# A gated DeltaNet block on one Trainium2 core: half-block norms, query norms and substitution rows issued at other places

## The chip, the core and the metric

The kernel runs on one core of one Trainium2 chip. The engines are TensorE (PE in the profile; its weight loads are PEld), VectorE (DVE), ScalarE (ACT), GpSimd (POOL) and SyncE (SP, which here issues most transfers). The metric is the device time of one execution in microseconds.

## The reference

One decoder layer over 2048 tokens of width 1024: RMS norm, a gated DeltaNet mixer of 8 heads of width 128, then a squared-ReLU MLP of width 4096, and a final norm. All in float32. The mixer, cut to what matters:

```python
proj = h @ w_in
qkv = silu(causal_depthwise_conv(proj[..., :3 * W], conv_w))       # 4 taps
q, k = l2_normalize(q), l2_normalize(k)                            # per head
beta = sigmoid(b);  g = -exp(a_log) * softplus(a + dt_bias)
# per head, chunks of 64 tokens, gc = cumsum(g) in the chunk
lower = strict_lower(einsum(k*beta, k) * decay)
u, w  = triangular_solve(lower + I, [v*beta, k*beta*exp(gc)])
attn  = causal(einsum(q, k) * decay)
for each chunk:                                                    # state S of 128 x 128
    v_new = u - w @ S
    o     = (q*exp(gc)) @ S + attn @ v_new
    S     = S * exp(g_last) + (k*exp(g_last - gc)).T @ v_new
o = rms(o) * norm_w * silu(z);  out = o @ w_out
```

## The kernel before

The tokens are worked in two blocks (`blk`) of 1024, each as two half blocks (`s`) of 512. A half block does the mixer for the 8 heads in four pairs (`h` = 0, 2, 4, 6); after both half blocks follow the out projection and the MLP of the block, which the change does not touch. So there are 16 pairs in all.

Float32 products run as three matmuls on high and low parts (L117 to L119), so a projection (`conv_part`) is 24 matmuls of 128x512. Weights are split on GpSimd (L90, L91) in block 0. A pair runs six projections (k, q, v for two heads, counted by `n`), each followed by its causal convolution on VectorE (L307, L311) with copies on ScalarE (L303, L304, L310). Between the projections stand steps of two pairs at once:

- For the pair itself: after n = 3 and 4 the key products (`key_matrices`, L429 to L439, tiles mt), then `invert_diagonal`: ScalarE copies four pieces of the triangular matrices into xc (L322), VectorE transposes them into pr (L325) and then substitutes row by row, 31 rows, each a multiply (L333, tmp) and a reduction (L335, tt). These rows are taken from a generator, `rows_of`, a few at a time.
- For the pair before (`prev`): `prepare2`, a generator of stages taken one by one through `next(stages)`. It inverts the triangular matrices from the 32-wide diagonal blocks up (`invert`: tr L345 is VectorE's transpose of the finished rows, tcm L347, then L365 to L394 on TensorE), then makes k and v per token (kt, vt: transposes L469 into po, ScalarE L472) and the attention matrix (L478, L480).

After the six projections `wind_up` does the rest of the pair before: two gate projections (z), the query norms (`query_norms`: squares sq on ScalarE L450, sums on TensorE L452, an addition n on VectorE L454), and `chain`, four steps of the state for two heads: k·S (L496), y (VectorE, L498), q·S (L502, into po), y times the inverse (L505), vr (ScalarE, L507), the state's update (L511, S L512), L515. Calls of `fill` in it take rows of `rows_of`, to fill VectorE's time.

During the first half block of a block, each pair also loads and norms one 128-row tile of the next half block's input (`norm_transpose`): the load xt, its squares on ScalarE, the reciprocal root on VectorE (`rstd_of`), the scaling xn (L181), then eight transposes on TensorE (L186, po) with high and low parts hh and hl.

The code states an order, but a scheduler then orders the instructions of each engine, and an engine takes its own strictly in that order. The three PSUM tags matter: kq and pj with three buffers, po with two. Four buffers (tag "xt") serve xt, xn, xc, pr and a gate's z2.

Of the kernel before, what the change touches and what calls it, by code (L numbers as in the profile page):

```python
# [16 lines left out]
P = 128  # L17
# [16 lines left out]
def tile_kernel(ctx: ExitStack, tc: tile.TileContext, x, w_in, w_out, w_up, w_down, n_mlp, n_fin, consts, out):  # L34
# [106 lines left out]
    def rstd_of(ssq, use_pool=False):  # L141

        n = ssq.shape[-1]
        m = sm.tile([P, n], F32, name="rm", tag=f"rm{n}")
        dve.tensor_scalar(m, ssq, 1.0 / D, EPS, op0=MULT, op1=ADD)  # L145
        r = sm.tile([P, n], F32, name="rst", tag=f"rst{n}", bufs=3)
        if use_pool:
            pool.tensor_tensor(r, m, mhalf, op=ALU.pow)
        else:
            rsqrt(r, m)  # L150
        return r
# [22 lines left out]
            dve.scalar_tensor_tensor(hl[:, k, :], ps, nmix[:, k:k + 1], hh[:, k, :].bitcast(F32),  # L174
                                     op0=MULT, op1=SUB)

    def norm_transpose(i, src, xn, wcol, hh, hl, tag):

        ssq = sm.tile([P, 1], F32, name="ssq", tag="ssq", bufs=3)
        act.activation(xn, src, AF.Square, accum_out=ssq)  # L180
        dve.tensor_scalar_mul(xn, src, rstd_of(ssq))  # L181
        ti = slice(i * P, (i + 1) * P)
        for k4 in range(0, KS, 4):
            ps = big(tag)
            for k in range(4):
                pe.transpose(ps[:, k * P:(k + 1) * P], xn[:, (k4 + k) * P:(k4 + k + 1) * P], ident)  # L186
# [259 lines left out]
    def query_norms(ap, u, q2, j):  # L446

        ps = big("kq")
        sq = ap.tile([P, HB], F32, name="sq", tag="scr", bufs=1)
        act.activation(sq, q2[:, j * HB:(j + 1) * HB], AF.Square)  # L450
        for t in range(HT):
            pe.matmul(ps[:, t:t + 1], sq[:, sl(t)], ones[:, 0:1], start=True, stop=True)  # L452
        c = NC + j * HT
        dve.tensor_scalar_add(u["n2"][:, c:c + HT], ps[:, 0:HT], 4.0 * EPS)  # L454

    def prepare2(ap, sb, h, q2, k2, v2, gt, u, ub, t64):

        c0 = h * HT
        dt_, rk = u["dt"], u["rk"]
        yield from invert(ap, u["mt"], u["tt"], ub, t64)  # L460
        yield
        qe = row(ap, eg_d, "qe", sb, c0)
        (dve if c0 == NH * HT - NC and sb % 2 else pool).tensor_tensor(flat(qe), flat(qe), q2, op=MULT)
        kt, vt = head(ap, "kt"), head(ap, "vt")
        for dst, src, sc in ((vt, v2, lambda c: rk[:, c:c + 1]), (kt, k2, lambda c: gt["egl"][:, c0 + c:c0 + c + 1])):
            for hf in range(2):
                ps = big("po")
                for t in range(HT):
                    pe.transpose(ps[:, sl(t)], src[:, sl(hf * HT + t)], ident)  # L469
                for t in range(HT):  # L470
                    c = hf * HT + t
                    act.activation(dst[:, c, :], ps[:, sl(t)], AF.Copy, scale=sc(c))  # L472
        yield
        for hf in range(2):
            ps = big("kq")
            for t in range(HT):
                s = sl(hf * HT + t)
                pe.matmul(ps[:, sl(t)], k2[:, s], q2[:, s], start=True, stop=True)  # L478
            cs = slice(hf * HT, (hf + 1) * HT)
            dve.tensor_tensor(flat(dt_[:, cs, :]), ps, flat(dt_[:, cs, :]), op=MULT)  # L480
        u.update(ub=ub, qe=qe, kt=kt, vt=vt, at=dt_, k2=k2, gt=gt, c0=c0)

    def chain(ap, h0, u, fill):

        def col(name, c):
            return u["gt"][name][:, u["c0"] + c:u["c0"] + c + 1]

        po = [big("po") for _ in range(HP)]
        for t in range(HT):
            ts_ = slice(t * P, (t + 1) * P)  # L490
            cs = [j * HT + t for j in range(HP)]
            st = [S[h0 + j] for j in range(HP)]
            ys, vrs = [], []
            for j, c in enumerate(cs):
                ps = big("kq")
                pe.matmul(ps[:, 0:P], u["k2"][:, c * P:(c + 1) * P], st[j], start=True, stop=True)  # L496
                y = ap.tile([P, P], F32, name="y", tag="y")
                dve.scalar_tensor_tensor(y, ps[:, 0:P], col("neg", c), u["vt"][:, c, :], op0=MULT, op1=ADD)  # L498
                ys.append(y)
            fill(3)  # L500
            for j, c in enumerate(cs):
                pe.matmul(po[j][:, ts_], u["qe"][:, c, :], st[j], start=True, stop=False)  # L502
            for j, c in enumerate(cs):
                ps = big("kq")
                pe.matmul(ps[:, 0:P], u["ub"][:, c, :], ys[j], start=True, stop=True)  # L505
                vr = ap.tile([P, P], F32, name="vr", tag="vr")
                act.activation(vr, ps[:, 0:P], AF.Copy, scale=u["cc"][:, c:c + 1])  # L507
                vrs.append(vr)
            for j, c in enumerate(cs):
                ps = big("kq")  # L510
                pe.matmul(ps[:, 0:P], u["kt"][:, c, :], vrs[j], start=True, stop=True)  # L511
                dve.scalar_tensor_tensor(st[j], st[j], col("egt", c), ps[:, 0:P], op0=MULT, op1=ADD)  # L512
            fill(2)
            for j, c in enumerate(cs):
                pe.matmul(po[j][:, ts_], u["at"][:, c, :], vrs[j], start=False, stop=True)  # L515
        os_ = [ap.tile([P, HT, P], F32, name="o", tag="o") for _ in range(HP)]
        ms = sm.tile([P, NC], F32, name="ms", tag="ms")
        for j in range(HP):
            for t in range(HT):
                c = j * HT + t  # L520
                act.activation(os_[j][:, t, :], po[j][:, t * P:(t + 1) * P], AF.Square, accum_out=ms[:, c:c + 1])
        nq = sm.tile([P, NC], F32, name="nq", tag="nq")
        dve.tensor_scalar_mul(nq, u["n2"][:, NC:2 * NC], EPS * P)
        dve.scalar_tensor_tensor(nq, ms, 1.0 / P, nq, op0=MULT, op1=ADD)
        rq = sm.tile([P, NC], F32, name="rq", tag="rq")
        rsqrt(rq, nq)
        for j in range(HP):
            for t in range(HT):
                c = j * HT + t
                act.activation(os_[j][:, t, :], po[j][:, t * P:(t + 1) * P], AF.Copy, scale=rq[:, c:c + 1])  # L530
        return os_
# [53 lines left out]
    def mixer(blk, hT):  # L585
        with tc.tile_pool(name="ap", bufs=2) as ap:
# [11 lines left out]
            def wind_up(stages, rows_of, sb, h, hT, qkv, gt, u):  # L598

                def fill(n):  # L600
                    for _ in range(n):
                        next(rows_of, None)

                fill(1)
                z = [gate(ap, hT, h, sb)]
                for _ in stages:
                    pass
                z.append(gate(ap, hT, h + 1, sb))
                for j in range(HP):
                    query_norms(ap, u, qkv[0], j)  # L610
                os_ = chain(ap, h, u, fill)
                return [(sb, h + j, os_[j], z[j]) for j in range(HP)]

# [4 lines left out]
            for s in range(2):  # L618
                sb = 2 * blk + s
                for h in range(0, NH, HP):  # L620
                    qkv, n = [], 0
                    stages = stages_of(*prev) if prev is not None else iter(())
                    next(stages, None)
                    if s == 0 and h == 0:
                        hT2 = half_tiles()
                    for part in (1, 0, 2):
                        d = ap.tile([P, HP * HB], F32, name=f"c{part}", tag=f"c{part}")
                        qkv.append(d)
                        for j in range(HP):
                            conv_part(ap, hT, part, h + j, d[:, j * HB:(j + 1) * HB], sb)  # L630
                            n += 1
                            next(stages, None)
                            if s == 0 and h == 0 and n <= 3:
                                if n == 1:
                                    gt = {}
# [12 lines left out]
                            if blk == 0 and s == 1 and n in (2, 5):  # L648
                                split_out(h // HP * 2 + n // 5)
                            if s == 0 and n == 1:  # L650
                                xt = wp.tile([P, D], F32, name="xt", tag="xt", bufs=4)
                                r0 = (sb + 1) * HB + h // HP * P
                                sp.dma_start(xt, x[r0:r0 + P, :])
                            if s == 0 and n == 2:
                                xt_steps = norm_transpose(
                                    h // HP, xt, wp.tile([P, D], F32, name="xn", tag="xt", bufs=4), nmix, *hT2, "po")
                            if s == 0 and n in (2, 4):
                                next(xt_steps)
                            if s == 0 and h == NH - HP and n >= 4:
                                if n == 4:  # L660
# [2 lines left out]
                                next(g_steps, None)  # L663
                    if prev is not None:
                        ready += wind_up(stages, rows_of, *prev)
                    for _ in rows_of:
                        pass
                    prev = sb, h, hT, (qkv[1], qkv[0], qkv[2]), gt, u
                if s == 0:
                    for _ in g_steps:  # L670
# [226 lines left out]
```

## Time and profile before

| | |
|---|---|
| median of 3 runs | 2931.71 us (2922.69 to 2936.09) |
| profiled execution | 2926.04 us, span 2924.3 us |
| mean granted clock of TensorE | 0.978 |
| busy: PE, DVE, ACT, POOL | 95%, 53%, 35%, 25% of the span |
| mixer of block 0 (28 to 655 us) and block 1 (1510 to 2075 us) | PE idle about 78 and 39 us |

Times are microseconds from the span's start. A line of the table of waits reads: engine, tile and line that waited, the engine, tile and line it waited for, then the total, the number of waits and the longest. In a window or timeline row the busy time stands with the number of instructions in brackets; the bracket at the end of a timeline row is the idle time ahead of it and what ended it. `po L186 <- DVE xn L181` is TensorE's transpose of the next half block's tile, which waits for VectorE's scaling.

### The profile page before, as it was taken

What the parts mean: (1) busy time and instruction counts of PE and PEld (TensorE: products, weight loads), DVE (VectorE), ACT (ScalarE), POOL (GpSimd) and SP (SyncE); (2) the same over time, 40 slices, a digit from 0 to 9 for tenths busy, and PEclk for the clock granted to TensorE, in tenths of its full rate; (3) what the DMA queues carried; (4) which work ended last, traced back from release to release, by engine and by line L of the source; (5) the groups of instructions that cost most, each with busy time, mean ns of one, the idle gap of its engine ahead of it and who ended that gap; (6) DMA issues with size and microseconds to landing.
All of it is one profiled execution on the core that took longest, in us unless ns stands there. A gap on an engine that the chain in (4) does not pass through costs nothing.

```text
span 2924.3 us, 40261 instructions
## 1 busy us (share of the span) xinstructions
PE 2768.4 (95%) x15352; PEld 2325.2 (80%) x15352; DVE 1548.9 (53%) x3846; ACT 1034.0 (35%) x2338; POOL 731.9 (25%) x646
## 2 busy tenths in 40 slices
PE   7688989999999999999998999999999999999998
PEld 6577777779888888888886778787888888888887
DVE  7777777763433233333487676766544333332335
ACT  3455555554221211211246655555423112112112
POOL 6334232110042332332211111111004323323321
PEclk9889999999999999999999999999999999999999
DMA  6544455456421111111253434434662111111111
GB/s 227 182 159 168 165 177 176 169 202 226 161 72 43 58 50 38 58 51 37 65 194 142 142 122 145 145 137 148 199 230 87 44 44 58 44 44 58 48 40 65
DMA packets 81842, 337.62 MB, mean 115 GB/s; under 512 B 8817, under 2 KB 17265, under 8 KB 60145
## 3 DMA queue, kind: packets, MB, share of 16 engines
q1 hardware_dynamic: 60528, 292.98, 29.9%
q10 hardware_dynamic: 21120, 42.08, 4.2%
q8 instruction: 120, 1.97, 0.3%
q14 instruction: 74, 0.60, 0.1%
HBM read 271.98 MB, written 63.05 MB: 115 GB/s over the span
## 4 chain that ended last, share of the span: by engine, by line
PE 65%; DVE 10%; ACT 7%; issue 2%; DMA 2%; ACTq 0%; POOL 0%; POOLq 0%; DVEq 0%
PE pj L117 11%; PE pj L118 11%; PE pj L119 11%; PE kq L118 8%; PE kq L119 8%; PE kq L117 8%; ACT xc L322 2%; DVE tmp L333 2%; DVE c L307 1%; DVE tt L335 1%; DMA orw<-o_d 1%; PE kq L505 1%; PE kq L511 1%; PE kq L496 1%; PE kq L429 1%
## 5 line engine op out<-in xcount | busy, mean ns | idle before, releaser
L117 PE MATMUL pj<-hh,w 128*128 128x512 f32 x2048 | 820.7, 401 | 0.7 <-ACT c L304 0.7
L118 PE MATMUL pj<-hh,w 128*128 128x512 f32 x2048 | 817.6, 399 | 0.0
L119 PE MATMUL pj<-hl,w 128*128 128x512 f32 x2048 | 812.5, 397 | 0.0
L119 PEld LDWEIGHTS pj<-hl,w 128*128 128x128 f32 x2048 | 389.6, 190 | 79.0 <-issue 0.6
L117 PEld LDWEIGHTS pj<-hh,w 128*128 128x128 f32 x2048 | 390.1, 190 | 78.2 <-ACT c L304 1.1
L118 PEld LDWEIGHTS pj<-hh,w 128*128 128x128 f32 x2048 | 391.5, 191 | 75.8 <-issue 0.4
L742 ACT ACTIVATE r<-pj 128x512 f32<-128x512 f32 x128 | 76.9, 601 | 1059.7 <-PE pj L119 1059.7
L119 PE MATMUL kq<-dl,uh 128*128 128x512 f32 x992 | 386.8, 390 | 0.0
L118 PE MATMUL kq<-dh,ul 128*128 128x512 f32 x992 | 386.7, 390 | 0.0
L117 PE MATMUL kq<-dh,uh 128*128 128x512 f32 x992 | 386.6, 390 | 0.0
L745 DVE TENSOR_TENSOR ul<-r,uh 128x512 fp32r<-128x512 f32 x128 | 128.7, 1006 | 480.4 <-ACT uh L744 480.4
L785 DVE TENSOR_TENSOR x<-kq,x 128x512 f32<-128x512 f32 x256 | 176.8, 691 | 225.8 <-PE kq L119 223.1
L307 DVE SCALAR_TENSOR_TENSOR c<-raw,cst,c 128x512 f32<-128x512 f32 x288 | 239.9, 836 | 76.9 <-ACT c L304 73.9
L90 POOL TENSOR_SCALAR w<-wr 128x1024 fp32r<-128x1024 f32 x106 | 114.9, 1084 | 602.8 <-PE pj L119 380.5
L91 POOL TENSOR_TENSOR w<-wr,w 128x1024 fp32r<-128x1024 f32 x106 | 263.8, 2489 | 7.1
L785 DVE TENSOR_TENSOR x1h<-kq,x1h 128x512 f32<-128x512 f32 x256 | 176.7, 691 | 155.7 <-PE kq L119 155.4
L90 POOL TENSOR_SCALAR dh<-wr 128x1024 fp32r<-128x1024 f32 x62 | 64.5, 1058 | 642.0 <-PE kq L118 614.3
L117 PEld LDWEIGHTS kq<-dh,uh 128*128 128x128 f32 x992 | 186.2, 188 | 40.4 <-DVE rm L145 1.4
L118 PEld LDWEIGHTS kq<-dh,ul 128*128 128x128 f32 x992 | 186.2, 188 | 39.4
L119 PEld LDWEIGHTS kq<-dl,uh 128*128 128x128 f32 x992 | 186.2, 188 | 38.8
L333 DVE TENSOR_TENSOR tmp<-tt,pr 128x2 f32<-128x2 f32 (+30 forms) x496 | 162.1, 327 | 9.9 <-POOL pr L326 0.5
L117 PE MATMUL pj<-w,hh 128*128 128x256 f32 x512 | 147.2, 287 | 8.2 <-DMA w<-wo 5.9
(305 smaller groups left out, 3840.5 us busy)
## 6 DMA issues: line engine op xcount, KB each, us to landing
w<-wi SPq DMA_DIRECT2D x96, 1024.0 KB, 4.9
wi<-w SPq DMA_DIRECT2D x32, 1024.0 KB, 4.8
wr<-in_w_up SPq DMA_DIRECT2D x64, 512.0 KB, 3.6
w<-wo SPq DMA_DIRECT2D x32, 1024.0 KB, 5.7
wr<-in_w_down SPq DMA_DIRECT2D x64, 512.0 KB, 3.6
wr<-in_w_in SPq DMA_DIRECT2D x32, 512.0 KB, 5.8
qe<-eg_d ACTq DMA_DIRECT2D x16, 512.0 KB, 3.8
o_d<-z2s ACTq DMA_DIRECT2D x32, 256.0 KB, 3.3
```

Source lines behind the costliest of these rows:

```text
L90: pool.tensor_scalar(dst_h, src, 1.0, 0.0, op0=MULT, op1=ADD)
L91: pool.tensor_tensor(dst_l, src, dst_h.bitcast(F32), op=SUB)
L117: pe.matmul(ps, ah, bh, start=first and i == 0, stop=False)
L118: pe.matmul(ps, al, bh, start=False, stop=False)
L119: pe.matmul(ps, ah, bl, start=False, stop=last and i == n - 1)
L307: dve.scalar_tensor_tensor(dst, raw[:, k:k + HB], cw[:, 4 * f + k:4 * f + k + 1], dst, op0=MULT, op1=ADD)
L322: act.copy(xc[r], mt[r, :, 32 * b:32 * b + 32].rearrange("p t i -> p i t").unsqueeze(2) .to_broadcast([32, 32, R, NC]))
L333: dve.tensor_tensor(tmp[:, 0:n, 0:i + 1], tt[:, 0:n, 0:i + 1], pr[:, i, 0:i + 1].unsqueeze(1).to_broadcast([P, n, i + 1]), op=MULT)
L335: dve.tensor_reduce(tt[:, 0:n, i], tmp[:, 0:n, 0:i + 1], axis=mybir.AxisListType.X, op=ADD)
L742: act.activation(r, ps, AF.Relu)
L745: dve.tensor_tensor(ul[:, hs], r, uh[:, hs].bitcast(F32), op=SUB)
L785: dve.tensor_tensor(dst, ps, dst, op=ADD)
```

## The change

Four edits. First, in a block's first half the load of the next half block's tile moves ahead of the pair's first projection; the squares, the root and the scaling follow n = 1 (before, n = 2), and the eight transposes follow n = 3 and 4, four at each (before, n = 2 and 4). In block 1 the root is a power on GpSimd in place of eight operations on VectorE. Second, the query norms move from `wind_up` into `prepare2`, between stages of the inversion. The empty stage between inversion and kt/vt goes, and so does the stage that was taken ahead of the first projection. Third, the first pair's rows are no longer used up at the end of that pair: 12 of them come after the second pair's first projection and 24 more calls after its second (its stages start one projection later). Fourth, the second `fill` in a state step takes three rows instead of two.

```diff
-        dve.tensor_scalar_mul(xn, src, rstd_of(ssq))
+        dve.tensor_scalar_mul(xn, src, rstd_of(ssq, use_pool))
+        yield
...
-        yield from invert(ap, u["mt"], u["tt"], ub, t64)
-        yield
+        for i, _ in enumerate(invert(ap, u["mt"], u["tt"], ub, t64)):
+            yield
+            if i in (1, 2):
+                query_norms(ap, u, q2, i - 1)
...
-            fill(2)
+            fill(3)
...
-                for j in range(HP):
-                    query_norms(ap, u, qkv[0], j)
                 os_ = chain(ap, h, u, fill)
...
-                    next(stages, None)
+                    if s == 0:
+                        xt = wp.tile([P, D], F32, name="xt", tag="xt", bufs=4)
+                        r0 = (sb + 1) * HB + h // HP * P
+                        sp.dma_start(xt, x[r0:r0 + P, :])
...
-                            next(stages, None)
+                            if s == 0 and h == HP and n < 3:
+                                for _ in range(12 * n):
+                                    next(rows_of, None)
+                            if not (s == 0 and h == HP and n == 1):
+                                next(stages, None)
...
-                            if s == 0 and n == 2:
                                 xt_steps = norm_transpose(
-                                    h // HP, xt, wp.tile([P, D], F32, name="xn", tag="xt", bufs=4), nmix, *hT2, "po")
-                            if s == 0 and n in (2, 4):
+                                    h // HP, xt, wp.tile([P, D], F32, name="xn", tag="xt", bufs=4), nmix, *hT2, "po",
+                                    blk > 0)
+                            if s == 0 and n in (1, 3, 4):
                                 next(xt_steps)
...
-                    for _ in rows_of:
-                        pass
+                    if prev is not None:
+                        for _ in rows_of:
+                            pass
```

The lines of the changed kernel lie one to three lower: L333 becomes L334, L335 L336, L450 L451, L452 L453, L454 L455, L472 L475, L496 L499, L498 L501, L505 L508.

How the scheduler then orders the engines is seen at three places. On VectorE, around the second pair of block 0: the scaling xn and the substitution rows of the first pair around it, before:

```order
137 L333 TENSOR_TENSOR tmp<-tt,pr 128x4x14
138 L139 SCALAR_TENSOR_TENSOR rst<-rt,rst 128x1
141 L333 TENSOR_TENSOR tmp<-tt,pr 128x4x15
142 L139 SCALAR_TENSOR_TENSOR rst<-rt,rst 128x1
144 L181 TENSOR_SCALAR xn<-xt,rst 128x1024
145 L333 TENSOR_TENSOR tmp<-tt,pr 128x4x16
```

and now:

```order
120 L334 TENSOR_TENSOR tmp<-tt,pr 128x2x6
121 L139 SCALAR_TENSOR_TENSOR rst<-rt,rst 128x1
124 L181 TENSOR_SCALAR xn<-xt,rst 128x1024
126 L334 TENSOR_TENSOR tmp<-tt,pr 128x2x7
128 L334 TENSOR_TENSOR tmp<-tt,pr 128x2x8
```

The last number of tmp grows by one with each row of the substitution, so xn stood ahead of the row with 16 and now stands ahead of the row with 7.

On VectorE again, in the second half of block 0, at the first state step of the pair h = 0, while the next pair's rows run, before:

```order
865 L333 TENSOR_TENSOR tmp<-tt,pr 128x5x18
866 L454 TENSOR_SCALAR n_3427<-kq 128x4
867 L335 TENSOR_REDUCE tt<-tmp 128x5
868 L333 TENSOR_TENSOR tmp<-tt,pr 128x5x19
869 L537 SCALAR_TENSOR_TENSOR z2s<-z2s,pj 128x512
870 L335 TENSOR_REDUCE tt<-tmp 128x5
871 L454 TENSOR_SCALAR n_3427<-kq 128x4
872 L333 TENSOR_TENSOR tmp<-tt,pr 128x5x20
873 L498 SCALAR_TENSOR_TENSOR y<-kq,neg,vt 128x128 x2
```

and now:

```order
870 L334 TENSOR_TENSOR tmp<-tt,pr 128x5x17
871 L336 TENSOR_REDUCE tt<-tmp 128x5
872 L334 TENSOR_TENSOR tmp<-tt,pr 128x5x18
873 L501 SCALAR_TENSOR_TENSOR y<-kq,neg,vt 128x128
874 L540 SCALAR_TENSOR_TENSOR z2s<-z2s,pj 128x512
875 L501 SCALAR_TENSOR_TENSOR y<-kq,neg,vt 128x128
876 L336 TENSOR_REDUCE tt<-tmp 128x5
```

The additions n are gone from this place; y stands two rows of the substitution further ahead than it did, where n stood.

On ScalarE, ahead of the same state step, the copies xc for the next pair and the vt and kt of this one, before:

```order
311 L322 COPY xc<-mt 32x1024
314 L472 ACTIVATE vt<-po,rk 128x128 x8
315 L472 ACTIVATE kt<-po,egl 128x128 x2
317 L472 ACTIVATE kt<-po,egl 128x128 x6
318 L322 COPY xc<-mt 32x1024
321 L322 COPY xc<-mt 32x1024 x2
```

and now:

```order
317 L475 ACTIVATE vt<-po,rk 128x128 x8
319 L475 ACTIVATE kt<-po,egl 128x128 x8
320 L323 COPY xc<-mt 32x1024 x3
323 L323 COPY xc<-mt 32x1024
```

The four copies xc, the first of which stood ahead of vt and kt, now all stand behind them.

More of the change, by code (lines that the diff above doesn't have):

```diff
@@ L175, in enter_first, with norm_transpose @@
                                      op0=MULT, op1=SUB)
-    def norm_transpose(i, src, xn, wcol, hh, hl, tag):
+    def norm_transpose(i, src, xn, wcol, hh, hl, tag, use_pool=False):
         ssq = sm.tile([P, 1], F32, name="ssq", tag="ssq", bufs=3)
         act.activation(xn, src, AF.Square, accum_out=ssq)
-        dve.tensor_scalar_mul(xn, src, rstd_of(ssq))
+        dve.tensor_scalar_mul(xn, src, rstd_of(ssq, use_pool))
+        yield
         ti = slice(i * P, (i + 1) * P)
@@ L650, in mixer @@
                             if s == 0 and n == 1:
-                                xt = wp.tile([P, D], F32, name="xt", tag="xt", bufs=4)
-                                r0 = (sb + 1) * HB + h // HP * P
-                                sp.dma_start(xt, x[r0:r0 + P, :])
-                            if s == 0 and n == 2:
                                 xt_steps = norm_transpose(
-                                    h // HP, xt, wp.tile([P, D], F32, name="xn", tag="xt", bufs=4), nmix, *hT2, "po")
-                            if s == 0 and n in (2, 4):
+                                    h // HP, xt, wp.tile([P, D], F32, name="xn", tag="xt", bufs=4), nmix, *hT2, "po",
+                                    blk > 0)
+                            if s == 0 and n in (1, 3, 4):
                                 next(xt_steps)
```

## The prediction

> **What bounds the kernel.** I read the page's busy times first, then TensorE's waits, then a table of windows by stage, and last the timelines of two places.
>
> ```profile
> span 2924.3 us, 40261 instructions
> PE 2768.4 (95%) x15352; PEld 2325.2 (80%) x15352; DVE 1548.9 (53%) x3846; ACT 1034.0 (35%) x2338; POOL 731.9 (25%) x646
> PE po L186 <- DVE xn L181: 27.2, 2, 16.0
> PE kq L496 <- DVE n L454: 21.6, 8, 5.5
> PE po L469 <- ACT vt L472: 13.3, 10, 5.1
> PE po L186 <- ACT o L530: 11.6, 4, 8.1
> PE kq L452 <- ACT sq L450: 11.6, 4, 3.2
> 28.00:312.00 284.00, 230.92 (x1375) 188.69 (x1373) 217.50 (x582) 140.16 (x305) 124.92 (x115) 0.89 0.50 174
> 312.00:655.00 343.00, 318.31 (x2037) 267.49 (x2038) 247.28 (x746) 180.59 (x431) 68.19 (x91) 0.96 0.53 181
> 1510.00:1750.00 240.00, 215.00 (x1369) 176.92 (x1367) 173.56 (x584) 140.88 (x310) 29.50 (x62) 0.96 0.41 145
> 1750.00:2075.00 325.00, 311.40 (x2046) 262.34 (x2046) 229.01 (x750) 180.25 (x432) 32.74 (x68) 0.98 0.42 146
> ```
>
> TensorE is busy 95% of the span, so the kernel can only gain where TensorE waits, or where its clock is cut. The waits (total, times, longest) that the change touches are the xn scaling, the query norms n with their squares sq, and o and vt, ScalarE's reads of the po buffers. The four windows (length, then busy PE, PEld, DVE, ACT, POOL, then the granted clock) are block 0's first and second half and block 1's; outside them stands the MLP, which is untouched. TensorE idles 284 − 230.92 = 53 us, 25, 25 and 14: about 117 us in the stages that change. There VectorE is busy 70 to 77%, so a wait on it can be a wait for throughput and not for order.
>
> **A settled pair (second half blocks).** The rows of one pair of block 1, between the fourth projection's end and the first state step:
>
> ```profile
> 1951.31 1.14 PE L392 MATMUL kq<-ub,z 64*64 64x64 f32 x16
> 1959.51 2.01 ACT L322 COPY xc<-mt 32x1024 f32<-32x1024 f32 x1 [3.35 <-DVE mt L439]
> 1962.48 2.09 ACT L472 ACTIVATE vt<-po,rk 128x128 f32<-128x128 f32 x8
> 1965.66 1.65 ACT L472 ACTIVATE kt<-po,egl 128x128 f32<-128x128 f32 x6
> 1967.33 1.99 ACT L322 COPY xc<-mt 32x1024 f32<-32x1024 f32 x1
> 1970.67 4.12 ACT L322 COPY xc<-mt 32x1024 f32<-32x1024 f32 x2
> 1974.83 1.25 DVE L325 STREAM_TRANSPOSE pr<-xc 128x1024 f32<-128x1024 f32 x1 [2.07 <-ACT xc L322]
> 1976.62 0.16 DVE L333 TENSOR_TENSOR tmp<-tt,pr 128x2 f32<-128x2 f32 x1
> 1979.83 0.39 PE L117 MATMUL pj<-hh,w 128*128 128x512 f32 x1
> 1980.06 0.39 PE L118 MATMUL pj<-hh,w 128*128 128x512 f32 x1
> 1982.78 0.95 PE L452 MATMUL kq<-ones,sq 128*128 128x1 f32 x8
> 1985.21 0.16 DVE L454 TENSOR_SCALAR n<-kq 128x4 f32<-128x4 f32 x1
> 1985.42 0.49 PE L496 MATMUL kq<-S,c 128*128 128x128 f32 x2 [1.36 <-DVE n L454]
> 1987.24 0.49 PE L505 MATMUL kq<-y,ub 128*128 128x128 f32 x2 [0.87 <-DVE y L498]
> ```
>
> The order of work before shows why n is late: it stands behind 17 rows of the substitution, from 1976.62 to 1985.21, and these behind pr, which ends the chain of four xc copies on ScalarE. The change takes n away, but in the new order the first y stands behind the same 17 to 18 rows (the fence on VectorE above). So the wait moves from n to y.
>
> Its size: without waits TensorE stood at L496 at 1985.42 − 1.36 = 1984.06, or 32.8 us after 1951.31. In the new order six projection matmuls (1980.06 − 1979.83 = 0.23 each, 1.4) and the two groups of norm sums (0.95 each, about 1.7 with their overlap) no longer stand ahead; the k·S and q·S matmuls (about 1.4) now do. It reaches the y product near 31.1 us. On the other side the first xc copy ran in an idle place of ScalarE (3.35 idle before it) and now stands behind vt and kt; the edit takes away the empty stage that let it in. I add 1.8 of its 2.01 to pr, take off the two n (0.3), and with the rows unchanged y is done about 36.0 us after 1951.31. The wait is 36.0 − 31.1 = 4.8 us instead of 1.36 + 0.87 = 2.2.
>
> A longer gap also costs behind its end (columns as in the windows above):
>
> ```profile
> 565.50:572.00 6.50, 5.74 (x22) 4.83 (x23) 4.73 (x20) 0.73 (x2) 0.00 (x0) 0.51 0.79 268
> 1985.20:1992.00 6.80, 5.71 (x40) 4.97 (x40) 6.35 (x26) 1.47 (x4) 0.00 (x0) 1.00 0.01 4
> ```
>
> The first stretch follows a gap of 3.9 us on n in block 0 (row below), the second the gaps of 1.36 and 0.87. Only the longer gap is followed by half clock; half of 5.74 busy us is about 2.8 us lost, and about 2.4 where the stretch is shorter.
>
> In block 0 GpSimd's weight splits hold VectorE up; the waits of the two second halves, block 0's first, stand behind:
>
> ```profile
> 560.00 2.37 POOL L91 TENSOR_TENSOR w<-wr,w 128x1024 fp32r<-128x1024 f32 x1
> 560.21 2.21 DVE L333 TENSOR_TENSOR tmp<-tt,pr 128x33 f32<-128x33 f32 x1
> ...
> PE kq L496 <- DVE n L454: 11.8, 3, 3.9
> PE kq L365 <- ACT z L367: 3.6, 4, 1.4
> ...
> PE kq L452 <- ACT sq L450: 2.7, 1, 2.7
> PE po L469 <- ACT vt L472: 2.3, 4, 0.6
> PE kq L365 <- ACT z L367: 2.3, 4, 0.7
> ```
>
> A row of some 0.2 us becomes 2.21 while the split runs. With one such stall (and 0.8 of smaller ones) between pr and y, y comes at 38.8 and the wait is 7.5, against 11.8/3 = 3.9 on n and, as in block 1, some 0.8 on y and vt. Against this, the norm sums between the inversion's steps fill the wait on z (0.9 a pair in block 0, 0.6 in block 1). Per settled pair, then: block 0, 7.5 − 4.7 − 0.9 = +1.9, at a clock that was cut before too; block 1, 2.6 − 0.6 (z) − 0.6 (vt) = +1.4, and +2.4 for the half clock that a gap of 4.8 brings and one of 1.36 did not, +3.8. Two pairs are settled in each half. The pair that enters the half I count −0.7 and +2.2 (the same y wait, less the 2.6 or so on sq, which goes), the last two together −0.2 and +0.6. Second halves: 3.8 − 0.7 − 0.2 = +2.9 and 7.6 + 2.2 + 0.6 = +10.4.
>
> A rule on the cut clock: the Trainium skill, "TensorE: Matmul & The Clock Gate", section "Part 1: The HAM clock gate", has the gate fall to half after at least one idle window of about 3.4 us, and full speed return after a like time of steady work. This trace agrees for the 3.9 us gap (0.51) and for 1.36 (1.00); by it 4.8 us always pays, but a wait that turns out at 3 us would not, and the 2.4 in each of two pairs would fall away: −4.8 on the sum.
>
> **The first pairs of a block.** Windows from pr to xn, xn to the end of the substitution, from there to the first state product; the last row is that third window in block 1:
>
> ```profile
> 77.90:98.70 20.80, 4.88 (x22) 3.71 (x20) 20.20 (x48) 8.24 (x18) 11.60 (x12) 0.72 0.51 194
> 98.70:130.60 31.90, 25.46 (x102) 20.66 (x103) 28.65 (x59) 11.62 (x31) 11.49 (x13) 0.82 0.56 190
> 130.60:162.90 32.30, 29.10 (x235) 24.39 (x235) 14.58 (x56) 19.48 (x29) 13.27 (x11) 0.92 0.45 163
> 1589.20:1619.60 30.40, 26.96 (x229) 22.57 (x228) 14.40 (x56) 18.84 (x27) 2.58 (x5) 0.95 0.35 122
> 149.16 8.11 ACT L322 COPY xc<-mt 32x1024 f32<-32x1024 f32 x4 [0.86 <-DVE mt L439]
> ```
>
> The two largest waits (16.0 and 11.3, 27.2 together) stand here on xn. The change lets xn come some 10 us sooner, because it stands behind 5 rows of the substitution and not 14 (counted in the two orders) and its norm begins a projection earlier. But VectorE is busy 20.20 of 20.80 and 28.65 of 31.90 us up to the end of the substitution, and its work there is the same set. What TensorE no longer waits for xn it then waits for the substitution's result. At most the 3.85 idle us come off; I take half, −2, and in block 1 −1.4. Behind it the gain is real: on TensorE's order 52 projection matmuls stand between that wait's matmul (L365) and the first k·S before, 33 now; the other 19 run ahead of it, 19 × 0.23 = 4.4 us off 29.10 busy; TensorE's work is 24.7, and ScalarE's chain there (12.5 of copies, then xc 8.11, pr, three rows, y) about 25. So −7.5 in block 0 and −5 in block 1. The next stretch gives −2.5 and −1 (VectorE nearly full again), the one after +0.7 and +2.5 (the 8.1 wait on o turns into one on the substitution, and xc falls behind vt and kt), the last 0 and +1. First halves: −11.3 and −3.9.
>
> **The rest.** fill(3) for fill(2) moves rows within the state steps, whose end is set by ScalarE and TensorE in turn: 0, and at worst four rows of 0.8 us. The x tiles' four loads of 512 KB stand earlier on SyncE's queue, ahead of one or two weight loads; weights wait for GpSimd, not for SyncE, so 0, at worst one load. GpSimd's power (rstd in block 1) replaces eight small VectorE operations:
>
> ```profile
> L148 POOL TENSOR_TENSOR rst<-rm,mhalf x20: 550/552/1466, 7.1 to 2919.3; 128x1 f32<-128x1 f32 x20
> ```
>
> 0.55 to 1.47 us each, three times, beside other work: between −1 and +4, I take 0. A rule that speaks against it: the Trainium skill, "SBUF — State Buffer", section "Who interferes with whom", says that a VectorE instruction with two SBUF inputs contends with a GpSimd one that reads SBUF, and is blocked for its length. The 2.21 us row above agrees for the split; for the power no run here shows it, and by the rule three times 0.55 us would be added to VectorE's 173.56.
>
> **Sum.** −11.3 + 2.9 − 3.9 + 10.4 = −1.9, say −2 us, from the profiled 2926 us. That execution lies 5.7 us under the median of 2931.7; on the median's footing I forecast 2930. Its own bounds: the first halves between −2 (only VectorE's idle comes off) and −27 (both waits on xn go), the second between 0 (the wait changes name only) and +20 (3.8 in five pairs): 2903 to 2950.
>
> **Rivals.**
> - *The waits named go.* xn 27.2, n 21.6, sq 11.6 and o 11.6 are 72 us in 18 waits, and if eight of these are followed by half clock at 2.5, 20 more: −92 at most. For it: ScalarE and GpSimd have room, and the waits on n are of order. Against: VectorE's 97% beside the 16 us wait, and the rows ahead of y. Half of it gives 2886.
> - *Slower: y behind the rows.* If y waits as worked out in all eight second-half chains and VectorE's fullness leaves the first halves at −2: 8 × 3.5 − 2 = +26 less two sq waits of 2.7, near 2952. It decides if y comes later than TensorE by more than 3 us, where the half clock sets in. For it: the new order of ScalarE. Against: in a chain where pr is early, 17 rows are done in time.
> - *It does nothing.* The same rows and copies pace both, and each wait only changes its name: ±5 us, near 2932; it is counted with the forecast.
>
> **How the numbers follow.** A change under 0.5% (14.7 us) is about what a measurement of this kernel can't tell from none. The forecast, together with the no-change rival, holds 0.46, inside that band but for its edges; the waits going 0.32, since 117 us of idle lie in the touched stages; the slower one 0.22. Of the forecast's tails 0.01 falls on either side: faster 0.33, same 0.44, slower 0.23. Half of each outer rival lies beyond its centre (0.16 below 2886, 0.11 above 2952), so a little more than both centres, 2886 to 2956, leaves out about 2 in 10.
>
> **What would show it.** Right: the wait on xn (27.2) shrinks to a few us while one on the substitution's result (L366, from L347's tcm) of over 10 appears in each first half; L499 no longer waits for n and L508 waits for y by 4 to 8 us in settled pairs, with the clock near 0.5 behind it in block 1; the window of 32.3 falls to 25. Wrong: total idle of TensorE falls by over 30 us (then VectorE was not the limit, and early xn freed it), or y is early since more rows fall behind it than the order shows; or a new wait on weights appears behind the x loads.

## The result

The changed kernel takes 2975.36 us (median of 4 runs, 2970.88 to 2977.57) against 2929.31 us before: a ratio of 1.0159, 95% interval 1.0138 to 1.0181. It is 46 us slower, where 2930 was forecast and 2956 was the range's upper end. From the page of the profile after:

```profile
span 2973.6 us, 40208 instructions
PE 2792.1 (94%) x15352; PEld 2352.1 (79%) x15352; DVE 1564.2 (53%) x3814; ACT 1031.1 (35%) x2338; POOL 736.1 (25%) x650
```

and, cut, from its table of TensorE's waits (total, times, longest):

```profile
PE kq L508 <- DVE y L501: 65.5, 13, 9.1
PE kq L366 <- ACT z L368: 21.1, 8, 5.2
PE po L472 <- DVE hl L191: 14.5, 3, 7.9
PE kq L366 <- ACT tcm L348: 11.6, 7, 3.1
PE po L187 <- ACT o L533: 5.5, 1, 5.5
PE po L472 <- ACT vt L475: 4.9, 4, 2.7
PE po L187 <- DVE xn L181: 4.0, 1, 4.0
```

Of the kernel before, beside the waits that the prediction shows:

```profile
PE kq L365 <- ACT z L367: 6.1, 9, 1.4
PE kq L365 <- ACT tcm L347: 4.3, 5, 1.9
PE kq L505 <- DVE y L498: 3.6, 7, 0.9
PE po L469 <- DVE hl L190: 1.3, 1, 1.3
```

The waits that the change aimed at are gone or small: xn is down from 27.2 to 4.0, n and sq are no longer there. In their place stand 65.5 us on y in 13 of the 16 chains of state steps, where y had 3.6, z with 21.1, where it had 6.1, and 14.5 on hl (L191, the low parts of the next half block's input) at L472, where L469 had 1.3. The span grew by 49.3 us; TensorE's busy time by 2792.1 − 2768.4 = 23.7 with the same 15352 matmuls, its idle time by the other 25.6.

Windows between first y products of chosen chains, of the kernel before and then of the one after (length, busy PE, PEld, DVE, ACT, POOL, granted clock):

```profile
28.00:339.10 311.10, 257.79 (x1515) 210.76 (x1513) 241.08 (x674) 151.92 (x337) 129.42 (x122) 0.90 0.49 171
339.10:684.10 345.00, 320.43 (x2182) 271.97 (x2182) 237.88 (x699) 187.71 (x462) 63.69 (x83) 0.96 0.55 188
684.10:1773.30 1089.20, 1055.53 (x5496) 884.58 (x5496) 519.00 (x1250) 331.43 (x721) 260.89 (x208) 0.99 0.29 95
1773.30:2102.30 329.00, 314.22 (x2183) 266.72 (x2182) 220.51 (x699) 187.88 (x462) 32.07 (x65) 0.98 0.45 153
```

```profile
28.00:340.80 312.80, 258.41 (x1498) 212.18 (x1496) 244.49 (x652) 150.20 (x337) 130.46 (x123) 0.90 0.48 168
340.80:699.20 358.40, 322.28 (x2166) 275.65 (x2166) 247.92 (x716) 187.52 (x462) 66.93 (x84) 0.94 0.52 177
699.20:1799.50 1100.30, 1066.95 (x5513) 896.15 (x5511) 515.32 (x1201) 330.60 (x720) 263.30 (x212) 0.98 0.29 94
1799.50:2146.50 347.00, 319.51 (x2168) 273.82 (x2166) 231.37 (x716) 187.64 (x462) 32.38 (x65) 0.96 0.41 144
```

Block 0's first half: +1.7. Its second half: +13.4, nearly all of it idle time (345.00 − 320.43 = 24.6 before, 36.1 after). The third window, the MLP and block 1's first half: +11.1, and none of it idle; busy time rose by 11.4. Cut once more, its first 866 us (to 1550.0 before and to 1565.0 after, nearly all MLP) are equal in length; the 11 us lie behind, in block 1's first half, where the clock falls from 0.96 to 0.93. Block 1's second half: +18.0, idle +12.7 and busy +5.3. The last 5.1 of the 49.3 us lie behind these windows, in block 1's MLP. So there are two losses: in second halves TensorE waits, in block 1's first half it works at a lower clock.

### The profile page after: what moved, and what is told of

It reads as the page before. It is cut to its first block, busy times and chain, and to the rows that moved or that the text cites. A ratio compares the mean times of both kernels' runs of the same rounds, so it can differ in the third digit from the quotient of the medians.

```text
span 2973.6 us, 40208 instructions
## 1 busy us (share of the span) xinstructions
PE 2792.1 (94%) x15352; PEld 2352.1 (79%) x15352; DVE 1564.2 (53%) x3814; ACT 1031.1 (35%) x2338; POOL 736.1 (25%) x650
## 4 chain that ended last, share of the span: by engine, by line
PE 70%; DVE 16%; ACT 8%; issue 2%; DMA 2%; POOL 1%; ACTq 0%; DVEq 0%; POOLq 0%; SPq 0%
PE pj L117 12%; PE pj L118 12%; PE pj L119 12%; PE kq L118 8%; PE kq L119 8%; PE kq L117 8%; DVE tmp L334 4%; ACT xc L323 3%; DVE c L308 3%; DVE tt L336 2%; DMA orw<-o_d 1%; PE kq L430 1%; PE kq L508 1%; PE kq L514 1%; PE kq L453 1%
## 5 line engine op out<-in xcount | busy, mean ns | idle before, releaser
L117 PEld LDWEIGHTS pj<-hh,w 128*128 128x128 f32 x2048 | 395.0, 193 | 80.1 <-POOL w L90 1.4
L118 PEld LDWEIGHTS pj<-hh,w 128*128 128x128 f32 x2048 | 394.7, 193 | 79.3 <-POOL w L91 3.1
L91 POOL TENSOR_TENSOR w<-wr,w 128x1024 fp32r<-128x1024 f32 x106 | 266.4, 2514 | 7.7
L90 POOL TENSOR_SCALAR w<-wr 128x1024 fp32r<-128x1024 f32 x106 | 112.4, 1060 | 591.7 <-PE pj L119 364.3
L90 POOL TENSOR_SCALAR dh<-wr 128x1024 fp32r<-128x1024 f32 x62 | 64.0, 1048 | 639.4 <-PE kq L118 611.3
L334 DVE TENSOR_TENSOR tmp<-tt,pr 128x2 f32<-128x2 f32 (+30 forms) x496 | 181.3, 365 | 11.1 <-POOL pr L327 0.5
```

Of the source, the lines that this page charges most:

```text
L90: pool.tensor_scalar(dst_h, src, 1.0, 0.0, op0=MULT, op1=ADD)
L91: pool.tensor_tensor(dst_l, src, dst_h.bitcast(F32), op=SUB)
L117: pe.matmul(ps, ah, bh, start=first and i == 0, stop=False)
L118: pe.matmul(ps, al, bh, start=False, stop=False)
L334: dve.tensor_tensor(tmp[:, 0:n, 0:i + 1], tt[:, 0:n, 0:i + 1], pr[:, i, 0:i + 1].unsqueeze(1).to_broadcast([P, n, i + 1]), op=MULT)
```

## The experiments

Ratios are against the kernel before, run beside each experiment; microseconds from them are taken on 2929. Each part was first done alone. Code is cut at the dots.

**The parts alone.** Norms of the queries, stages and the empty stage together:

```diff
-        yield from invert(ap, u["mt"], u["tt"], ub, t64)
-        yield
+        for i, _ in enumerate(invert(ap, u["mt"], u["tt"], ub, t64)):
+            yield
+            if i in (1, 2):
+                query_norms(ap, u, q2, i - 1)
...
-                for j in range(HP):
-                    query_norms(ap, u, qkv[0], j)
...
-                    next(stages, None)      # ahead of the first projection
```

> Only the second edit: query norms between the inversion's stages, the empty stage and the stage ahead of the first projection gone; the loads, the norms, the first pair's rows and fill stay as before. Theory 1 (the second edit makes the loss: the inversion starts one projection later, TensorE then waits for z and tcm, and y stands where n stood): +30 to +45 us on 2930, waits of L366's kind on z and tcm over 20 us and on y over 45 us. Rival (the loss comes from the first halves, where the norms and the first pair's rows were moved): within 15 us of before.

Measured: 1.0199 (1.0174 to 1.0224), +58 us, more than the 30 to 45 of theory 1, with its waits: 57.5 on y, 20.5 on z, 4.6 on tcm. The second edit alone loses somewhat more than the whole change (the two intervals just overlap). Which part of it?

```diff
-                    next(stages, None)      # l_only: this line alone
```

> Only the stage ahead of a pair's first projection is taken away; query norms stay in wind_up and the empty stage stays. Theory 1 with the stage's shift as its cause: +10 to +25 us, z and tcm waits up by 10 us or more, n waits about as before. Theory 1 with the query norms as its cause: within 8 us.

Measured: 1.0016 (0.9999 to 1.0033), +5 us. My first theory after the result put the blame on this shift of the inversion; alone, the shift costs nothing clear of noise. It does move waits, against what I expected: those on n fall from 21.6 to 4.0 and those on vt rise from 13.3 to 37.9. The norms alone, with both stages kept:

```diff
-        yield from invert(ap, u["mt"], u["tt"], ub, t64)
+        for i, _ in enumerate(invert(ap, u["mt"], u["tt"], ub, t64)):
+            yield
+            if i in (1, 2):
+                query_norms(ap, u, q2, i - 1)
         yield
...
-                for j in range(HP):
-                    query_norms(ap, u, qkv[0], j)
```

> Only the query norms move between the inversion's stages; both empty places of stages stay as before. Theory 1 with the norms as its cause: +15 or more, y waits replace n at 4 to 7 us a pair. With the stage's shift as its cause: between -20 and +10 us, and the xc copies keep their place ahead of vt and kt, so y waits of under 3 us a pair.

Measured: 1.0166 (1.0144 to 1.0189), +49 us. Its largest waits of TensorE among those that matter here:

```profile
PE kq L508 <- DVE y L501: 57.5, 10, 10.3
PE po L186 <- DVE xn L181: 23.9, 2, 15.5
PE kq L365 <- ACT tcm L347: 18.9, 9, 6.2
```

The move of the norms alone replaces n by y. The first edit alone (load, scaling, transposes, power on GpSimd):

> Only the first edit: loads ahead of the first projection, scaling after n = 1, transposes after n = 3 and 4, power on GpSimd in block 1. Theory 1: -10 to 0 us, the waits on xn fall from 27 to under 12 us and a part comes back as waits on the substitution's result. Rival (first halves lose): +10 to +25 us.

Measured: 1.0040 (1.0024 to 1.0056), +12 us: the time falls into the rival's range (first halves lose). The wait on xn falls to 12.1, those on vt and tcm rise by 7.6 and 3.6, and idle time stays at 155 us. Then the whole change without the norms' move:

> The whole change but the query norms, which stay in wind_up ahead of the state steps; the stages' shift, the norms of the next half block, the first pair's rows and fill(3) are as in the change. If the query norms' move alone makes the loss: 2915 to 2940, waits on y under 10 us in total and waits on n back near 20. If the parts work together: 2945 or more.

Measured: 1.0062 (1.0040 to 1.0084), +18 us, or 2947: just in the range of the parts working together, while the waits are those of the other theory (n 25.6, y 7.6) and z has 22.8. So the norms' move, 49 us alone, adds 28 to the other edits. The whole change without the second edit:

> The first, third and fourth edit without the second (norms of the next half block, first pair's rows, fill(3)). If the first pairs of a block gain what I forecast for them (-11 and -4 us): 2905 to 2918. If VectorE's throughput there lets nothing through: within 8 us of before.

Measured: 1.0056 (1.0042 to 1.0071), +16 us, outside both ranges. From its page:

```profile
span 2944.3 us, 40230 instructions
PE 2799.1 (95%) x15352; PEld 2350.8 (80%) x15352; DVE 1555.6 (53%) x3814; ACT 1028.9 (35%) x2338; POOL 735.7 (25%) x650
```

Idle time is 2944.3 − 2799.1 = 145 us, 11 less than before. That is near the 15 that I forecast for the first halves; but busy time is 30.7 longer. The first pair's rows alone, and the fourth edit alone:

```diff
...
+                            if s == 0 and h == HP and n < 3:
+                                for _ in range(12 * n):
+                                    next(rows_of, None)      # c_only
...
-            fill(2)
+            fill(3)                                          # d_only
```

> Only the first pair's rows spread over the second pair's first two projections (its inversion starts one stage later for that). Theory that VectorE is full there: -5 to +8 us, the wait on xn shrinks because fewer rows stand ahead of it and comes back as waits on tcm. Rival that the order of rows sets the 16 us wait: -15 us or better.

> Only fill(3) in place of fill(2). My sum had 0 and at worst +3: within 5 us of before.

Measured: 1.0037 (1.0022 to 1.0052), +11 us, just outside both ranges, and 0.9993 (0.9975 to 1.0011), nothing. The wait on xn in the former stayed at 26.7, and tcm rose from 4.3 to 11.8. VectorE's timeline shows the same 14 rows ahead of xn as before, so this run does not say whether fewer rows would bring xn sooner. Where 5 rows stand ahead of it, in the changed kernel and in the one without the second edit, it waits 4.0 and 3.6 us, but there its norm starts sooner too.

**Why the norms' move costs.** The same norms left out of the kernel before, with a constant in n2:

> The kernel before with the query norms left out altogether (their squares, sums and additions; a constant stands in their place). Theory 2 (what is lost is the place of the norms: before, they and some projection matmuls stood ahead of the first state step and filled the time that the substitution needs; without them TensorE comes to y early and stands): 10 to 45 us slower than before although it does less, with waits on y of 4 to 7 us a pair. Rival (the norms at their new place delay the inversion): 5 to 30 us faster than before.

Measured: 1.0061 (1.0042 to 1.0081): 18 us slower with less to do. Its page and, behind it, its waits:

```profile
PE 2756.5 (94%) x15096; PEld 2312.8 (79%) x15096; DVE 1557.5 (53%) x3814; ACT 1013.1 (34%) x2306; POOL 733.1 (25%) x662
```

```profile
PE kq L506 <- DVE y L499: 51.2, 11, 8.6
PE kq L365 <- ACT tcm L347: 20.6, 11, 4.6
```

Nearly the same waits on y as with the norms moved (57.5 in 10). TensorE's idle time is 188.6 us here, 186.4 with the norms moved and 155.8 before; the busy time is 25 us shorter than with the norms moved, with their 256 matmuls gone. So the loss of idle time does not need the norms at their new place; it is enough that they are gone from the old one. Next, one small VectorE write (the diagonal of pr, which is 1.0 already) takes a y as input, and the substitution's rows from the K-th on have to wait for it:

```diff
...
                 ys.append(y)
+            if t == 0 and pr is not None:
+                dve.tensor_scalar(pr[:, K, K:K + 1], ys[1][:, 0:1], 0.0, 1.0, op0=MULT, op1=ADD)
```

> The changed kernel with one small VectorE write after the first two y, which the substitution's rows from the 12th on have to wait for; so y stands behind 11 rows and not 16. Theory 2: y comes about 3 us earlier, the y waits fall by half to two thirds, 15 to 30 us come back; the end of the substitution is later by less than it has room. Rival (the inversion is what is late): under 8 us come back.

> As the run with 12, from the 8th row on: y behind 7 rows. Theory 2: y waits under 1.5 us a pair, 25 to 50 us come back against the changed kernel, unless the later end of the substitution then makes tcm late (waits on tcm over 3 us a pair). Rival: under 8 us.

Measured: 1.0121 (1.0097 to 1.0145) and 1.0074 (1.0053 to 1.0096), that is 11 and 25 us back from the changed kernel's 1.0159: the fewer rows ahead of y, the less is lost. Both lie above the rival's 8 us, the former below the 15 to 30 of theory 2, the latter at the edge of its 25 to 50. From the waits of the run with 8:

```profile
PE kq L367 <- ACT tcm L349: 38.9, 14, 8.2
PE kq L511 <- DVE y L502: 25.4, 9, 6.2
```

y falls from 65.5 to 25.4, and tcm, the substitution's result, rises from 11.6 to 38.9. But z, which stands at the same place and had 21.1, no longer waits: together the two go from 32.7 to 38.9, so 6 of the 40 us that y gives back are asked again at the end of the rows. TensorE's idle time falls by 30 us to 151, which is less than before the change; only 25 us come back, and the kernel stays slower than the one before, because the busy time is longer (2796.8 against 2768.4; the clock is treated below). The same write on the norms' move alone:

> The query norms' move alone, with the write that holds the substitution's rows from the 8th on behind the first two y. If the loss of that move (+48) is y's place behind the rows: 30 to 50 us come back, within 15 us of before. If the norm sums between the inversion's stages cost by themselves: under 25 come back.

Measured: 1.0083 (1.0064 to 1.0102), so 24 of its 49 us come back. That is the rival's range (under 25) and not the 30 to 50 of y's place as the whole cause, though the noise of the two runs, some 9 us, doesn't part them. Its waits on y fell from 57.5 to 20.6 us, those on z and tcm rose from 19.9 to 27.2 and those on o from 10.4 to 18.6: the hold itself costs elsewhere. So the run shows about half of the move's loss in the rows ahead of y and doesn't say what the rest is; the run without the norms speaks against the rival. And on the kernel before:

> The kernel before with the same write, from the 12th row on: n and y stand behind 11 rows and not 16 to 20. Theory 2: the waits on n (21.6) fall below 8 us and the half clock behind them goes, 10 to 30 us faster than before. If the end of the substitution has no room: within 8 us.

> The kernel before with the substitution's rows from the 16th on held behind the first two y: n and y behind 15 rows and not 16 to 20. If there is room: 5 to 15 us faster than before, n waits of 21.6 down to about 15 and tcm waits not above 8. If what is taken from n comes back at tcm, as with 12: within 5 us.

Measured: 1.0000 (0.9987 to 1.0013) and 1.0014 (1.0005 to 1.0023). With 12, the waits on n and tcm are

```profile
PE kq L366 <- ACT tcm L348: 23.6, 10, 3.1
PE kq L497 <- DVE n L455: 6.9, 4, 4.7
```

where they were 21.6 (n) and 4.3 (tcm). z, 6.1 before, no longer waits, so the end of the rows asks 23.6 where it asked 10.4, and the waits on o at L186 rise from 11.6 to 21.1. In the kernel before, what is taken from n comes back at tcm and o, and idle time stays (155.8 and 152.2 us); no version here beats it beyond the noise.

**The clock.** Idle matmuls, as many as fit into the wait, directly ahead of the first y product:

```diff
...
+                if t == 0 and j == 0:
+                    for _ in range(warm):
+                        pe.matmul(ps[:, P:2 * P], u["ub"][:, c, :], u["k2"][:, c * P:(c + 1) * P], start=True, stop=True)
```

> The changed kernel with 14 to 60 idle matmuls of 128x128 (their result is overwritten) directly ahead of the first y product in 12 chains, so many as fit into the wait measured there less about 1 us. Theory of the clock: waits stay the same in length if the idle matmuls are left out of the count, the half clock behind the y gaps goes, 15 to 30 us come back (2945 to 2960). Rival (the clock is cut for another reason, or the gap itself is the whole loss): between -3 and +10 us against the changed kernel.

Measured: 1.0439 (1.0419 to 1.0460). I had reckoned 0.11 us for one; a float32 128x128 stands in the trace as two instructions of 0.11 us, 45 matmuls took 10 us, and they overran the waits. With half as many:

> As after_warm with half as many idle matmuls (7 to 32 of 0.23 us, ahead of the first y product in 12 chains), which now end about 1 us before y is there. Theory of the clock: the stretches behind the y waits run at 1.0 instead of about 0.7, 10 to 25 us come back against the changed kernel (2950 to 2965). Rival (the gap alone is the loss, or the clock falls for another reason): -3 to +10 us.

Measured: 1.0241 (1.0218 to 1.0264), slower than the changed kernel. The scheduler answered the added matmuls with another order on VectorE: the y of the second state step stand behind 23 to 28 rows in seven chains, where it was 17 to 20, and a new wait on the state S (28.7 in 12) appears. As a test of the total it failed: TensorE is busy 150.7 us at half clock, as in the changed kernel (150.2). What it shows is local; two windows of block 0 behind the first y product in the changed kernel, and then, in this run, the same two and the stretch that follows the new wait:

```profile
505.10:512.00 6.90, 6.90 (x35) 6.23 (x36) 4.53 (x18) 1.47 (x4) 0.00 (x0) 0.70 0.68 232
582.80:589.70 6.90, 6.89 (x32) 6.23 (x33) 4.30 (x16) 1.22 (x4) 0.00 (x0) 0.64 0.65 228
```

```profile
510.73:517.60 6.87, 2.37 (x14) 1.90 (x14) 6.29 (x22) 0.73 (x2) 0.00 (x0) 0.94 0.64 231
593.03:599.90 6.87, 2.37 (x14) 1.89 (x14) 6.29 (x22) 0.73 (x2) 0.00 (x0) 0.91 0.63 229
517.70:524.50 6.80, 6.77 (x32) 6.48 (x33) 4.20 (x14) 0.73 (x2) 0.00 (x0) 0.57 0.00 0
```

With the gap of 6.6 us filled down to 1.7 the stretch behind it has 0.91 to 0.94 and not 0.64 to 0.70. TensorE works for only 2.37 us of that stretch, as the new gap of 4.26 us lies in it; the half clock comes 6 us after the y product, and the stretch behind that gap has 0.57. By the rule of the Trainium skill, "TensorE: Matmul & The Clock Gate", section "Part 1: The HAM clock gate", an idle window of about 3.4 us brings the half clock; these three gaps agree with it. Others do not: in the kernel before, a gap of 2.55 us (on sq, up to 640.0) is followed by 6.8 us at a clock of 0.50, so here shorter gaps can bring it too. Another run fills the two waits on xn in the kernel before:

```diff
...
+            for _ in range(warm if k4 == 0 else 0):      # 58 in block 0, 40 in block 1
+                pe.matmul(ps, wh[:, 0, 0:P], wh[:, 0, :], start=True, stop=True)
```

> The kernel before with 58 and 40 idle matmuls of 128x512 in the two waits on xn (16.0 and 11.3 us). Theory of the clock: half clock of 17.1 and 10.2 us there goes, 6 to 12 us faster than before. Rival (VectorE sets the end of that stretch, so a faster TensorE only waits longer): within 4 us.

Measured: 1.0061 (1.0038 to 1.0085), 18 us slower, against both theories. Here too the order changed, and VectorE's timeline at the first pair's substitution shows how:

```profile
76.50 1.25 DVE L327 STREAM_TRANSPOSE pr<-xc 128x1024 f32<-128x1024 f32 x1 [1.40 <-ACT xc L324]
...
111.90 0.44 DVE L347 STREAM_TRANSPOSE tr<-tt 128x256 f32<-128x256 f32 x1
```

From pr to tr it is 35.4 us, where it was 52.7, and VectorE is busy 33.8 of them, where it was 48.8: part of its other work stood behind the rows. So the run says nothing clean of the clock, but it takes away my ground for the first halves.

## Why the prediction was wrong

The four terms were −11.3, +2.9, −3.9 and +10.4; the windows above, cut at about the same places, give +1.7, +13.4, +11.1 and +18.0. Two steps failed. The norm sums were to fill the wait on z, and that wait grew instead: z and tcm together from 10.4 to 32.7 us. And the y wait with its half clock was priced in second halves alone, while the first halves were to gain 15 us: y waits 21 us in the first halves too, and over the kernel the half clock makes TensorE's busy time 23.7 us longer, where the sum had 4.8 in block 1's settled pairs. By its steps:

- *The wait moves from n to y.* Right, and well sized. In TensorE's timeline at two settled pairs, one of each block:

```profile
505.07 0.58 PE L508 MATMUL kq<-y,ub 128*128 128x128 f32 x1 [6.62 <-DVE y L501]
...
1953.06 0.58 PE L508 MATMUL kq<-y,ub 128*128 128x128 f32 x1 [4.14 <-DVE y L501]
```

  6.6 and 4.1 us against the 7.5 and 4.8 forecast (36.0 − 31.1 is 4.9, a slip). Behind the former the window shown above has a clock of 0.70; behind the latter it is 0.75 for 6.9 us, so the half clock came, at 1.7 us lost where I had reckoned 2.4.
- *The norm sums fill the wait on z.* This step failed. I took 0.9 and 0.6 us a pair off; instead the wait doubled or more:

```profile
533.39 0.37 PE L366 MATMUL kq<-tcm,mt 32*32 32x32 f32 x6 [2.01 <-ACT z L368]
```

  Over the kernel, z and tcm went from 10.4 to 32.7 us, +22. The norm sums stand behind this wait in the new order and not ahead of it. This is the largest miss among the waits. And z itself is not later in the settled pairs: from the first products of the inversion (the first group of L366) to the second, which wait for z, it was 6.5 to 7.3 us and is 6.7 to 7.4. But 17 projection matmuls stand between them where 22 stood, and five of them, at 0.23 each, make 1.15 of the 1.3 us by which the wait grew there. So here too the filler went away. The wait on z does not come from the norms' move: with the whole second edit z waits 20.5 us, with the change less the norms' move 22.8, with the stage's shift alone 4.7, without any of the second edit 8.9, and with the norms' move alone it is tcm that waits (18.9). So it goes with the empty stage, alone or together with the other; I had not weighed it, and the empty stage alone was not run.
- *y in the first halves.* I priced the new wait in second halves only. It stands in the first pairs too:

```profile
159.37 0.58 PE L508 MATMUL kq<-y,ub 128*128 128x128 f32 x1 [5.67 <-DVE y L501]
```

  and again 8.7, 2.7 and 4.4 us in the next chains of first halves, 21 us together, against the −7.5 and −5 that I had there.
- *The window of 32.3 falls to 25.* It came to 31.3 (128.1 to 159.4). The projection matmuls did move ahead of the wait, but TensorE ran at a lower clock, 0.82 where the window before had 0.92, and then stood 5.7 us for y:

```profile
128.10:153.70 25.60, 25.59 (x211) 21.23 (x209) 10.07 (x43) 17.25 (x27) 8.93 (x7) 0.82 0.43 146
```

- *VectorE's throughput ends the substitution.* The time from pr to tr did stay, 52.5 after 52.7, and the wait for xn did turn into others (the 16.0 and 5.1 us on xn and vt became 4.0 on xn, 8.0 on hl and 2.7 on vt). They are not the one that I had named: no wait on tcm is longer than 3.1 us. And the reason was wrong: the run with idle matmuls ahead of xn has 35.4 us with another order. VectorE was full because the scheduler had put other work between the rows.
- *A cost of the clock for each gap.* I counted it for the settled pairs of block 1 alone. The trace's clock records have stretches at 1.0 and at 0.5. TensorE is busy 88.5 us at half clock in the kernel before, in 18 stretches, and 150.2 us after, in 34: half of the difference is 31 us, beside the 23.7 by which busy time rose. Busy time less that half lies between 2714 and 2725 us in all 15 kernels here with these 15352 matmuls, so the rise of the busy time is the half clock. The first edit, alone, leaves idle time as it was (155.8 and 155.1) and is busy 108.4 us at half clock, in 25 stretches. So the prediction's picture "a wait only changes its name" was right on idle time for that edit, not for the whole change (idle +25.6), and it missed that waits of 3 to 8 us are followed by a slow stretch of their own. Of the gaps of 3 us or more, 12 before and 18 after, 11 and 18 have half clock within 3.5 us of their end; of those of 2 to 3 us, 3 of 5 and 8 of 11. That more gaps are the cause of the whole rise is not shown: filling a gap was tried with a clean answer at two places only, and the kernel without the second edit has only 10 gaps of 3 us or more and is busy 158.5 us at half clock.
- *The rest.* fill(3) cost nothing, as forecast. The weights' wait that I named as a sign appeared, small: 2.5 us on w of GpSimd's L91 and 0.9 on L90. The power on GpSimd was not tried alone; it runs four times (GpSimd's instructions go from 646 to 650), where the prediction has three.

The slower rival had the mechanism (y behind the rows in nearly all chains) and came to 2952. It lacked z and tcm, and the clock in the first halves; I gave it 0.22. What stays open: why the parts don't add up (those tried alone come to 49 + 5 + 12 + 11 = 77 us with fill(3) at 0, and the whole is 46), what the empty stage does alone, what sets the half clock where no gap of 3 us stands ahead of it, and how much of the 46 filling the gaps would return.

## What to carry to other kernels

Where an in-order engine waits, look at what stands between its arrival and the wait: work that looks like a burden there may be the filler, and moving it away only exposes the wait (here +49 us for moving the norms, and +18 us even for leaving them out). Before shortening a wait, ask whether the two ends share one loop: in the kernel before, taking rows away from ahead of n gave 15 us there and took 13 at z and tcm. And read the clock beside the idle time: the first edit left idle time at 155 us, but the busy time at half clock went from 88.5 to 108.4 us and the kernel became 12 us slower.

## What the runs showed of the hardware

A float32 128x128 matmul stands in the trace as two instructions of 0.11 us each (90 for 45 in the run with idle matmuls); I had taken one. The granted clock is 1.0 or 0.5 in every run here, and a stretch at 0.5 lasts 3.41 us or a multiple of it, up to seven (but for the last one, which the end of the trace cuts). Filling a wait of 6.6 us down to 1.7 kept the next 6 us at full clock, where the changed kernel had half clock behind its wait. And 58 idle matmuls of 128x512 took 13.3 us, 0.23 each, at full clock from 79.2 on, as the projections do.
